# A decoder layer on one core: the queue model behind the emission order counts GpSimd's hold on VectorE and takes measured matmul times

## The chip, the cores and the metric

The kernel runs on one core of a Trainium2 chip. The metric is the device time of one execution in microseconds (us). The engines are named as the profile names them: PE (TensorE matmul) and PEld (its weight load), DVE (VectorE), ACT (ScalarE), POOL (GpSimd) and SP, which issues all the DMAs of this kernel. Each engine works through a queue of its own, in order; they meet only at semaphores.

## What is computed

One step of a decoder layer, for a prompt of 512 tokens and 8 samples that share the weights (520 columns). Cut to what matters:

```python
def mix_layer(x, ...):
    z = rms_norm(x, norm_g) @ w_in                  # 2048 x 7168, fp32
    u, gate_pool, qkv, gate_dil, q_mem, gate_mem = split(z)
    y_pool = pool_mix(u)                             # trailing means over 2/4/8/16, a 128x128 map per group
    for gi, (win, dil) in enumerate(((128, 1), (512, 4), (2048, 16))):
        q, k, v = rms_norm(q), rms_norm(k), v        # 4 heads in each of 3 groups
        o[gi], lse[gi] = dilated attention           # prompt: within 512 tokens; sample: over a cache
    y_dil = sum_g softmax_g(lse) * o                 # the groups of a head merged by their denominators
    y_mem = attention into 256 memory tokens         # its k and v come from mem @ w_mem_kv
    y = [silu(gate_pool)*y_pool | silu(gate_dil)*y_dil | silu(gate_mem)*y_mem]
    return x + y @ w_out                             # 1536 x 2048
```

The caches of the samples (88 MB) are copied to the outputs with one row added, from HBM to HBM.

## The kernel before

**Products in three parts.** Every fp32 product with a weight is made of three fp32r products, hi*hi, hi*lo and lo*hi. A column block of a weight (128 outputs) is a job; `run_jobs` (line 409) runs its 16 row blocks k (12 for w_out), each with three products over two halves of 260 columns, so six matmuls a step. The weights arrive in `wraw` tiles. `emit_split` (line 387) splits a quarter of a job (four row blocks): ACT rounds it to `whi` (line 154 of `act`) and DVE subtracts to get `wlo` (line 164 of `d_tt`). There are 304 such splits; they are counted here from 0. Five tiles of each kind exist (`SPB`, line 342), and a split is issued at the end of a quarter, three quarters ahead of its use, so that a `wlo` that DVE finishes late stops PE.

**Jobs.** In order: four of q_mem with the norm of x alongside; q and k of head 0 for two groups; eight of w_mem, with one half of 256 columns each (12 matmuls a quarter in place of 24); the gates; then for each head three v jobs and the q and k jobs of the next groups; the gate and the u of the pooled branch; and 16 of w_out, the first two of them together, k by k.

**Tasks.** All other work lies in generators: `norm_task` (line 501) of q and k, `mem_attn` (688), `dil_attn` (721), `sample_scores` (810), `sample_values` (833), `pool_task` (918). Each yields between steps. Sums and maxima over the 128 partitions are `partition_all_reduce` on POOL (`p_ar`, line 196): of squares `sq`, of a sample's scores `sk` (768 columns for a dilated unit, 512 for a memory one), of maxima and denominators `mx`.

**What sets the order.** The program is written out by a planner. `Clock` keeps a model of each engine's time: `use` (line 79) adds an instruction's estimated length to its engine, after what it reads and writes; the estimates stand in the helpers. After each row block `tick` (line 237) looks at the tasks in turn. A task's next step is emitted only when the model's PE has passed the time at which the step before is done, plus 1 us; nothing is emitted while the model has DVE or ACT more than 2.5 us ahead of PE in work (`busy`, line 234). So the estimates, not the chip, decide behind which split a step is put in the queue of its engine. For the first two w_out jobs `need_split` (line 1184) drives the tasks until the part of y that block k reads is split.

Names in the rows below: `sk`, `sv` are a sample unit's keys and values, `smx` its maximum, `sz` its denominator, `ss` and `sy` small tiles of the same unit, `qk` a q or k tile, `S` the prompt's scores of a head, `y4` to `y7` the gated outputs of the four dilated heads, `y0` to `y3` the gates of the pooled branch, `xl` and `xh` the two parts of x and later of y, `vn` a tile of v or of the residual x.

Of the kernel before, what the change touches and what calls it, by code (L numbers as in the profile page):

```python
# [10 lines left out]
F32 = mybir.dt.float32  # L11
# [37 lines left out]
class Clock:  # L49


    LAT = 0.12

    def __init__(self):
        self.pe = 0.0
        self.free = {"act": 0.0, "dve": 0.0, "pool": 0.0, "sp": 0.0, "hbm": 0.0}
        self.last = 0.0
        self.written = {}
        self.used = {}

    def after(self, ins, outs):
        t = 0.0
        for a in ins:
            t = max(t, self.written.get(a.tensor.name, 0.0))
        for a in outs:
            t = max(t, self.used.get(a.tensor.name, 0.0))
        return t
# [8 lines left out]
            self.written[n] = t  # L76
        self.last = max(self.last, t)

    def use(self, eng, dur, ins, outs):
        if eng == "pe":  # L80
            dep = max([self.written.get(a.tensor.name, 0.0) for a in ins])
            self.pe = max(self.pe, dep) + dur
            end = self.pe
            for a in ins:
                n = a.tensor.name
                self.used[n] = max(self.used.get(n, 0.0), end)
            for a in outs:
                n = a.tensor.name
                self.written[n] = max(self.written.get(n, 0.0), end + self.LAT)
                self.used[n] = max(self.used.get(n, 0.0), end)  # L90
            self.last = max(self.last, end + self.LAT)
            return
        end = max(self.free[eng], self.after(ins, outs)) + dur
        self.free[eng] = end
        self.done(end + self.LAT, ins, outs)

    def dma(self, nbytes, ins, outs):
        s = max(self.free["sp"], self.after(ins, outs)) + 0.57
        self.free["sp"] = s
        end = max(self.free["hbm"], s + 0.8) + nbytes / 345e3  # L100
        self.free["hbm"] = end
        self.done(end + 3.0, ins, outs)
# [5 lines left out]
def nfree(ap):  # L108
    n = 1
    for s in ap.shape[1:]:  # L110
        n *= s
    return n


def trunk(ctx, tc, nc, I, O):
    ck = Clock()
# [64 lines left out]

    def d_red(out, in_, op, axis):
        nc.vector.tensor_reduce(out=out, in_=in_, op=op, axis=axis)  # L183
        ck.use("dve", nfree(in_) * 0.00104 + 0.08, [in_], [out])

    def d_ttr(out, in0, in1, op0, op1, init, accum):
        nc.vector.tensor_tensor_reduce(out=out, in0=in0, in1=in1, scale=1.0, scalar=init, op0=op0, op1=op1,  # L187
# [3 lines left out]

    def d_recip(out, in_):
        nc.vector.reciprocal(out=out, in_=in_)
        ck.use("dve", nfree(out) * 0.0083 + 0.08, [in_], [out])

    def p_ar(t, op=RADD):
        nc.gpsimd.partition_all_reduce(t, t, P, op)  # L197
        ck.use("pool", nfree(t) * 0.00625 + 0.35, [t], [t])

    def p_tt(out, in0, in1, op):  # L200
        nc.gpsimd.tensor_tensor(out=out, in0=in0, in1=in1, op=op)
# [2 lines left out]
    def mm(out, lhsT, rhs, start, stop):  # L204
        nc.tensor.matmul(out, lhsT=lhsT, rhs=rhs, start=start, stop=stop)  # L205
        n = nfree(rhs)
        d = 2 * max(0.107, n / 1200.0) if lhsT.dtype == F32 else max(0.107, (n + 6) / 2400.0)
        ck.use("pe", d, [lhsT, rhs], [out])

    def tr(out, in_):  # L210
# [198 lines left out]
    def run_jobs(group, each=None, before=None):  # L409
# [13 lines left out]
        for k in range(nkb):  # L423
            if before:
                before(k)
            for j in group:
                _, _, lhs, sections, _, _ = jobs[j]
                if k % 4 == 0:
                    cur[j] = split_t.pop((j, k))
                whi, wlo = cur[j]  # L430
                mh, ml = lhs(k)
                for a, b, w, m in ((0, 0, whi, mh), (0, 1, whi, ml), (1, 0, wlo, mh)):
                    for s, (c0, c1) in enumerate(sections):
                        mm(accs[j][s], w[:, k % 4, :], m[:, c0:c1],
                           start=(k == 0 and a == 0 and b == 0), stop=(k == nkb - 1 and a == 1))
            if each:
                each(k)
            if k % 4 == 3:
                for _ in group:
                    emit_split()  # L440
            if flags.get("x"):
                while pend and (flags.get("mem") or pend[0][0]):
                    pend.pop(0)[1]()
            tick()
# [24 lines left out]
    def run_last(j):  # L469

        t = psum_m()
        xr = xres.pop(j - first_o)
        o = row("tmp", 3)
        for s, (c0, c1) in enumerate(SEC):
            acc = t[:, s, 0:c1 - c0]
            for k in range(KO):
                whi, wlo = split_t[j, k - k % 4]
                mh, ml = xs(k)
                for n, (w, m) in enumerate(((whi, mh), (whi, ml), (wlo, mh))):
                    mm(acc, w[:, k % 4, :], m[:, c0:c1], k == 0 and n == 0, k == KO - 1 and n == 2)  # L480
                if k == 0:
                    flush_pend()
            d_tt(o[:, c0:c1], acc, xr[:, c0:c1], ALU.add)
            store(O["o_y"][j - first_o][:, c0:c1], o[:, c0:c1])
# [16 lines left out]
    def norm_task(z, w, gcol, after):  # L501

        yield from take("sq")
        sq = row("sq", 2)[:, 0:w]
        act(sq, z, AF.Square)
        yield
        p_ar(sq)
        yield
        yield from rsqrt_steps(sq, P)
        d_stt(z, z, gains_r[:, gcol - GC_DQ:gcol - GC_DQ + 1], sq, ALU.mult, ALU.mult)  # L510
        give("sq")
        yield
        after()
# [174 lines left out]
    def mem_attn(h):  # L688
# [10 lines left out]
        d_tt(m, a[1], s[:, 0, :], ALU.max)  # L699
        yield  # L700
        p_ar(m, RMAX)
        yield
        d_tt(s[:, 0, :], s[:, 0, :], m, ALU.subtract)
# [9 lines left out]
        for kk in range(2):  # L713
            mm(o, vmem[h][:, kk * P:(kk + 1) * P], s[:, kk, :], kk == 0, kk == 1)
        yield
        p_ar(u)
        yield
        yield from finish_y(Y[8 + h][:, 0:SEQ], o, u)
# [131 lines left out]
    def sample_mem(h, bq, kx, vx):  # L850
        bs = slice(2 * bq, 2 * bq + 2)
        kv = kx.rearrange("p (b j) -> p b j", b=2)
        vv = vx.rearrange("p (b j) -> p b j", b=2)
        mx = st([P, 2], "smx", 2)
        z = st([P, 2], "sz", 2)
        y = st([P, 2], "sy", 2)
        d_red(mx, kv, ALU.max, AX.X)
        d_ts(mx, mx, -SCALE, ALU.mult)
        yield
        for b in range(2):  # L860
            act(kv[:, b, :], kv[:, b, :], AF.Exp, scale=SCALE, bias=mx[:, b:b + 1], accum=z[:, b:b + 1])
        yield
        d_recip(z, z)
        for b in range(2):
            d_ttr(vv[:, b, :], vv[:, b, :], kv[:, b, :], ALU.mult, ALU.add, 0.0, y[:, b:b + 1])
        d_tt(ysm[:, h, bs], y, z, ALU.mult)
# [3 lines left out]
    def sample_self(h):  # L870
        ss = st([P, NG, NS], "ss", 2)
        nself = st([P, NS], "nself", 2)
        d_tt(ss, qs[:, h], cs[:, :, :, 0, h], ALU.mult)
        yield
        p_ar(ss.rearrange("p g b -> p (g b)"))
        yield
        d_red(nself, ss.rearrange("p g b -> p b g"), ALU.max, AX.X)
        d_ts(nself, nself, -SCALE, ALU.mult)
        yield
        selfs[h] = (ss, nself)  # L880

    def sample_dil(h, bq, kx, vx):
        ss, nself = selfs[h]
        bs = slice(2 * bq, 2 * bq + 2)
        kv = kx.rearrange("p (g b j) -> p g b j", g=NG, b=2)
        vv = vx.rearrange("p (g b j) -> p g b j", g=NG, b=2)
        mx = st([P, 2], "smx", 2)
        z = st([P, 2], "sz", 2)
        zs = st([P, 2], "szs", 2)
        y = st([P, 2], "sy", 2)  # L890
        y2 = st([P, 2], "sy2", 2)
        d_red(mx, kv.rearrange("p g b j -> p b g j"), ALU.max, AX.XY)
        d_stt(mx, mx, -SCALE, nself[:, bs], ALU.mult, ALU.min)
        yield
        for b in range(2):
            act(kv[:, :, b, :], kv[:, :, b, :], AF.Exp, scale=SCALE, bias=mx[:, b:b + 1], accum=z[:, b:b + 1])
            c = 2 * bq + b
            act(ss[:, :, c], ss[:, :, c], AF.Exp, scale=SCALE, bias=mx[:, b:b + 1], accum=zs[:, b:b + 1])
        yield
        d_tt(z, z, zs, ALU.add)  # L900
        d_recip(z, z)
        d_tt(ss[:, :, bs], ss[:, :, bs], cs[:, :, bs, 1, h], ALU.mult)
        d_red(y2, ss[:, :, bs].rearrange("p g b -> p b g"), ALU.add, AX.X)
        for b in range(2):
            d_ttr(vv[:, :, b, :], vv[:, :, b, :], kv[:, :, b, :], ALU.mult, ALU.add, y2[:, b:b + 1], y[:, b:b + 1])
        d_tt(y, y, z, ALU.mult)
        ys = Y[4 + h][:, SEQ + 2 * bq:SEQ + 2 * bq + 2]
        d_tt(ys, ys, y, ALU.mult)
# [124 lines left out]
    for g, (w, d) in enumerate(WINS):  # L1033
        a, n, e = D2D[g]
# [292 lines left out]
```

## Time and profile before

| | |
|---|---|
| median of 3 runs | 927.62 us (927.02 to 927.92) |
| profiled execution, device time | 927.79 us |
| its span, first to last instruction | 926.0 us |
| mean granted clock | 0.992 |
| PE busy | 894.7 us (97%) |
| DVE busy | 672.9 us (73%) |
| ACT busy | 388.2 us (42%) |
| POOL busy | 285.0 us (31%) |

The profiled execution lies 0.2 us above the median of the runs, and its span 1.8 us below its device time. The table's shares are means over stages with different limits. What counts is where PE, the engine with hardly a gap, does stop, and on which engine's queue the thing stands that it waits for.

### The profile page before, as it was taken

To read this page: it belongs to the slowest core of one execution; us is meant where nothing else is said; L and a number is where in the kernel's file an instruction comes from. 1 tells how busy PE (TensorE), PEld (TensorE's weight loads), DVE (VectorE), ACT (ScalarE), POOL (GpSimd) and SP (SyncE) were. 2 spreads that over 40 slices of the span, in tenths; PEclk is the share of its full clock that TensorE was granted. 3 is DMA by queue.
4 is the path that set the end of the run, shared out by engine and by line. 5 is a ranking of instruction groups with operands and counts; after the bars stand their busy time and mean duration, and the time that the engine had idled before them with its cause. 6 is when DMAs were issued, how large, how long until landed. Compare 5 with 4: busy or idle time off the path is not lost.

```text
span 926.0 us, 17968 instructions
## 1 busy us (share of the span) xinstructions
PE 894.7 (97%) x7208; PEld 879.2 (95%) x7208; DVE 672.9 (73%) x1225; ACT 388.2 (42%) x795; POOL 285.0 (31%) x96
## 2 busy tenths in 40 slices
PE   7999898999999999999999999989999999999998
PEld 7999888999999999999998999989999899999998
DVE  7678999757888769977698866997659698333231
ACT  7547655443364434444343353245432624222220
POOL 1032544325444424622255322552215220000000
PEclk9999999999999999999999999999999999999999
DMA  9435346897877866578866788668975545899531
GB/s 347 157 114 196 115 154 224 270 341 233 275 222 258 289 223 212 195 260 311 289 233 217 271 300 311 218 221 285 332 253 195 211 137 197 329 389 352 196 104 47
DMA packets 64211, 219.52 MB, mean 237 GB/s; under 512 B 8440, under 2 KB 22648, under 8 KB 61944
## 3 DMA queue, kind: packets, MB, share of 16 engines
q1 hardware_dynamic: 64128, 218.39, 68.4%
q8 instruction: 56, 0.92, 0.4%
q14 instruction: 27, 0.22, 0.1%
HBM read 200.32 MB, written 106.25 MB: 331 GB/s over the span
## 4 chain that ended last, share of the span: by engine, by line
PE 70%; DVE 22%; ACT 3%; issue 3%; DMA 2%; POOL 0%; SPq 0%; DVEq 0%; ACTq 0%
PE psm L205 62%; PE psb L205 8%; DVE wlo L164 7%; DVE sv L187 3%; DVE mx L164 2%; DVE S L164 2%; DVE smx L183 1%; DVE sk L164 1%; ACT whi L154 1%; ACT sk L154 1%; DVE tmp L168 1%; DMA o_kv<-vt 1%; DVE vt L164 1%; DVE qk L164 1%; DVE smx L168 1%
## 5 line engine op out<-in xcount | busy, mean ns | idle before, releaser
L205 PE MATMUL psm<-xh,whi 128*128 128x260 f32 x2088 | 434.0, 288 | 9.2 <-ACT whi L154 8.4
L205 PE MATMUL psm<-xh,wlo 128*128 128x260 f32 x2088 | 426.2, 285 | 9.7 <-DVE wlo L164 9.7
L205 PE MATMUL psm<-xl,whi 128*128 128x260 f32 x2088 | 423.9, 284 | 0.0
L205 PEld LDWEIGHTS psm<-xh,whi 128*128 128x128 f32 x2088 | 326.2, 190 | 16.1 <-ACT whi L154 8.6
L164 DVE TENSOR_TENSOR wlo<-wraw,whi 128x512 fp32r<-128x512 f32 x304 | 270.4, 906 | 96.5 <-ACT whi L154 96.1
L205 PEld LDWEIGHTS psm<-xh,wlo 128*128 128x128 f32 x2088 | 324.8, 190 | 12.1 <-DVE wlo L164 12.0
L205 PEld LDWEIGHTS psm<-xl,whi 128*128 128x128 f32 x2088 | 324.4, 190 | 0.0
L154 ACT ACTIVATE whi<-wraw 128x512 fp32r<-128x512 f32 x304 | 181.0, 621 | 169.0 <-PE psm L205 149.3
L197 POOL PARTITION_ALL_REDUCE sk<-sk x32 | 130.3, 4071 | 130.3 <-DVE sk L164 56.1
L197 POOL PARTITION_ALL_REDUCE sq<-sq x32 | 101.0, 3164 | 186.2 <-ACT sq L154 186.2
L154 ACT ACTIVATE sk<-sk,smx 128x256 f32<-128x256 f32 (+1 forms) x64 | 35.5, 555 | 115.3 <-DVE smx L168 64.8
L197 POOL PARTITION_ALL_REDUCE mx<-mx x17 | 46.4, 2729 | 69.7 <-DVE mx L164 69.3
L164 DVE TENSOR_TENSOR tmp<-psm,vn 128x260 f32<-128x260 f32 x30 | 11.5, 424 | 76.8 <-PE psm L205 58.5
L154 ACT ACTIVATE tmp<-tmp 128x520 f32<-128x520 f32 (+2 forms) x76 | 46.3, 610 | 23.8 <-DVE sq L168 16.5
L154 ACT ACTIVATE sq<-qk 128x520 f32<-128x520 f32 x28 | 17.7, 636 | 85.9 <-DVE qk L164 77.9
L205 PE MATMUL psb<-y,wlo 128*128 128x256 f32 x128 | 37.7, 295 | 6.9 <-DVE wlo L164 6.9
L205 PE MATMUL psb<-y,whi 128*128 128x256 f32 x192 | 42.6, 290 | 0.8 <-ACT whi L154 0.8
L154 ACT ACTIVATE tmp<-sq,eps 128x520 f32<-128x520 f32 (+1 forms) x32 | 22.3, 696 | 33.2 <-POOL sq L197 33.2
L205 PEld LDWEIGHTS psb<-y,whi 128*128 128x128 f32 x192 | 32.9, 196 | 1.0 <-ACT whi L154 1.0
L187 DVE CUSTOM_DVE_ANT_1 sv<-sv,sk,sy 128x384 f32<-128x384 f32 x32 | 33.1, 1071 | 0.6
L205 PEld LDWEIGHTS psb<-y,wlo 128*128 128x128 f32 x128 | 24.9, 194 | 8.9 <-DVE wlo L164 8.8
L168 DVE SCALAR_TENSOR_TENSOR tmp<-sq,tmp 128x520 f32<-128x520 f32 (+1 forms) x32 | 21.6, 675 | 11.6 <-ACT tmp L154 11.6
(129 smaller groups left out, 740.8 us busy)
## 6 DMA issues: line engine op xcount, KB each, us to landing
o_cache<-cache SPq DMA_DIRECT2D x88, 712.0 KB, 7.9
wraw<-w_in SPq DMA_DIRECT2D x104, 512.0 KB, 5.3
o_cache<-cache SPq DMA_DIRECT2D x24, 584.0 KB, 6.6
vn<-xT SPq DMA_DIRECT2D x32, 260.0 KB, 5.7
wraw<-w_mem SPq DMA_DIRECT2D x16, 512.0 KB, 4.0
wraw<-w_out SPq DMA_DIRECT2D x14, 512.0 KB, 6.5
o_zero<-zero SPq DMA_DIRECT2D x6, 1024.0 KB, 8.8
sk<-dks SPq DMA_DIRECT2D x16, 384.0 KB, 3.0
```

Of the source, the lines that this page charges most:

```text
L154: nc.scalar.activation(out=out, in_=in_, func=func, scale=scale, bias=bias, **kw)
L164: nc.vector.tensor_tensor(out=out, in0=in0, in1=in1, op=op)
L168: nc.vector.scalar_tensor_tensor(out=out, in0=in0, scalar=scalar, in1=in1, op0=op0, op1=op1)
L183: nc.vector.tensor_reduce(out=out, in_=in_, op=op, axis=axis)
L187: nc.vector.tensor_tensor_reduce(out=out, in0=in0, in1=in1, scale=1.0, scalar=init, op0=op0, op1=op1, accum_out=accum)
L197: nc.gpsimd.partition_all_reduce(t, t, P, op)
L205: nc.tensor.matmul(out, lhsT=lhsT, rhs=rhs, start=start, stop=stop)
```

## The change

Three things in the planner's model; no instruction is added or taken away, and no tile changes its size.

1. `hold` is new. Each `p_ar` tells the model a stretch in which POOL's sum holds DVE: from 0.00563 us a column plus 0.1 us ahead of the sum's end, to 1.15 us ahead of it. If the model's DVE still has work queued at the stretch's start, the stretch's length is added to its time; an instruction that would start inside the stretch starts at its end. Reductions, reciprocals and instructions that read PSUM (tiles named `ps...`) are let through.
2. The length of a sum is 0.00563 us a column plus 0.35 us, before 0.00625 us.
3. A matmul of n columns takes n * 0.000456 + 0.0015 us in the model, before (n + 6) / 2400. For 260 columns that is 0.1201 us, before 0.1108 us.

```diff
     def use(self, eng, dur, ins, outs, shared=True):
...
-        end = max(self.free[eng], self.after(ins, outs)) + dur
+        start = max(self.free[eng], self.after(ins, outs))
+        if eng == "dve" and shared and not any(a.tensor.name.startswith("ps") for a in ins):
+            for s, e in self.held:
+                if s <= start < e:
+                    start = e
+        end = start + dur
         self.free[eng] = end
         self.done(end + self.LAT, ins, outs)
+
+    def hold(self, s, e):
+
+        if s < self.free["dve"]:
+            self.free["dve"] += e - s
+        self.held = [h for h in self.held if h[1] > self.pe] + [(s, e)]
...
     def p_ar(t, op=RADD):
         nc.gpsimd.partition_all_reduce(t, t, P, op)
-        ck.use("pool", nfree(t) * 0.00625 + 0.35, [t], [t])
+        ck.use("pool", nfree(t) * 0.00563 + 0.35, [t], [t])
+        e = ck.free["pool"]
+        ck.hold(e - nfree(t) * 0.00563 - 0.1, e - 1.15)
...
-        d = 2 * max(0.107, n / 1200.0) if lhsT.dtype == F32 else max(0.107, (n + 6) / 2400.0)
+        d = 2 * max(0.107, n / 1200.0) if lhsT.dtype == F32 else max(0.107, n * 0.000456 + 0.0015)
```

Of the 305 stretches of DVE's queue between two splits, 200 hold other instructions than before or hold them in another order; on ACT it is 147. Three places show how. Lines 164, 168, 179 and 183 of before are lines 177, 181, 192 and 196 of after.

DVE in the first dilated head, before, from split 137 (`wlo_751`) to split 139 (`wlo_764`):

```order
L164 TENSOR_TENSOR wlo_751_4897<-wraw_682_4381,whi_750_4896 128x512
L168 SCALAR_TENSOR_TENSOR tmp_749_4880<-sq_735_4786,tmp_749_4880 128x520
L168 SCALAR_TENSOR_TENSOR sq_735_4786<-tmp_749_4880,tmp_748_4879 128x520
L168 SCALAR_TENSOR_TENSOR qk_734_4783<-qk_734_4783,gains_r_3_66,sq_735_4786 128x520
L164 TENSOR_TENSOR wlo_754_4931<-wraw_697_4469,whi_753_4930 128x512
L164 TENSOR_TENSOR qk_756_4941<-psm_733_4776,rsx_9_72 128x260 x2
L183 TENSOR_REDUCE smx_758_4952<-sk_722_4681 128x2
L168 SCALAR_TENSOR_TENSOR smx_758_4952<-smx_758_4952,nself_674_4310 128x2
L179 COPY qs_19_82<-qk_734_4783 128x8
L164 TENSOR_TENSOR wlo_764_4973<-wraw_697_4469,whi_763_4972 128x512
```

After, from split 137 (`wlo_746`) to split 139 (`wlo_754`), and the first instruction behind it:

```order
L177 TENSOR_TENSOR wlo_746_4869<-wraw_682_4382,whi_745_4868 128x512
L177 TENSOR_TENSOR wlo_750_4908<-wraw_695_4461,whi_749_4907 128x512
L177 TENSOR_TENSOR qk_752_4918<-psm_730_4760,rsx_9_72 128x260 x2
L177 TENSOR_TENSOR wlo_754_4940<-wraw_695_4461,whi_753_4939 128x512
L177 TENSOR_TENSOR sz_736_4819<-sz_736_4819,szs_737_4820 128x2
```

The three steps of a norm (`tmp`, `sq`, `qk`) and the maximum of a sample unit (`smx`) no longer stand between these splits; both come behind split 141. The unit's values (`sz`, `sv`, `sy`), which stood ahead of split 137, now begin behind 139.

ACT at the gates of the pooled branch, before, from split 242 (`whi_1248`) to split 243 (`whi_1252`):

```order
L154 ACTIVATE whi_1248_8901<-wraw_1187_8436 128x512
L154 ACTIVATE sk_1216_8659,sz_1244_8883<-sk_1216_8659,smx_1243_8882 128x3x128
L154 ACTIVATE ss_1188_8439,szs_1245_8884<-ss_1188_8439,smx_1243_8882 128x3
L154 ACTIVATE sk_1216_8659,sz_1244_8883<-sk_1216_8659,smx_1243_8882 128x3x128
L154 ACTIVATE ss_1188_8439,szs_1245_8884<-ss_1188_8439,smx_1243_8882 128x3
L154 ACT_TABLE_LOAD
L154 ACTIVATE y0_1184_8409<-y0_1184_8409 128x520
L154 ACTIVATE y1_1205_8576<-y1_1205_8576 128x520
L154 ACTIVATE y2_1231_8752<-y2_1231_8752 128x520
L154 ACTIVATE y3_1251_8912<-y3_1251_8912 128x520
L160 ACT_TABLE_LOAD
L154 ACTIVATE whi_1252_8942<-wraw_1187_8436 128x512
```

After, from split 242 (`whi_1243`) on, with split 243 (`whi_1247`) in the second row:

```order
L167 ACTIVATE whi_1243_8890<-wraw_1192_8451 128x512
L167 ACTIVATE whi_1247_8923<-wraw_1192_8451 128x512
L167 ACTIVATE whi_1255_8961<-wraw_1201_8537 128x512
L167 ACTIVATE whi_1257_8992<-wraw_1201_8537 128x512
L167 ACTIVATE sk_1221_8718,sz_1251_8949<-sk_1221_8718,smx_1250_8948 128x3x128
L167 ACTIVATE ss_1185_8420,szs_1252_8950<-ss_1185_8420,smx_1250_8948 128x3
L167 ACTIVATE sk_1221_8718,sz_1251_8949<-sk_1221_8718,smx_1250_8948 128x3x128
L167 ACTIVATE ss_1185_8420,szs_1252_8950<-ss_1185_8420,smx_1250_8948 128x3
L167 ACTIVATE whi_1260_9028<-wraw_1213_8610 128x512
L167 ACTIVATE whi_1264_9069<-wraw_1213_8610 128x512
L167 ACTIVATE whi_1267_9100<-wraw_1218_8679 128x512
L167 ACT_TABLE_LOAD
```

Four exponentials of a sample unit and the two table loads with the four gates between them stood ahead of split 243. Now splits 243 to 245 come ahead of the exponentials, and 246 to 248 ahead of the table load.

DVE near the end of the w_mem jobs, before, from split 62 (`wlo_354`) to split 63 (`wlo_360`):

```order
L164 TENSOR_TENSOR wlo_354_1988<-wraw_306_1732,whi_353_1987 128x512
L168 SCALAR_TENSOR_TENSOR tmp_351_1969<-sq_325_1838,tmp_351_1969 128x256
L168 SCALAR_TENSOR_TENSOR sq_325_1838<-tmp_351_1969,tmp_350_1968 128x256
L168 SCALAR_TENSOR_TENSOR kmem0_11_74<-kmem0_11_74,gains_r_3_66,sq_325_1838 128x256
L164 TENSOR_TENSOR vt_356_1998<-psb_336_1890,mx_10_73 128x256
L164 TENSOR_TENSOR wlo_360_2017<-wraw_306_1732,whi_359_2016 128x512
```

After, around split 63 (`wlo_357`):

```order
L196 TENSOR_REDUCE smx_348_1968<-sk_297_1676 128x2
L187 TENSOR_SCALAR smx_348_1968<-smx_348_1968 128x2
L177 TENSOR_TENSOR vt_355_1983<-psb_333_1879,mx_10_73 128x256
L177 TENSOR_TENSOR wlo_357_1996<-wraw_307_1735,whi_356_1995 128x512
L177 TENSOR_TENSOR wlo_360_2014<-wraw_312_1773,whi_359_2013 128x512
L181 SCALAR_TENSOR_TENSOR tmp_352_1974<-sq_325_1830,tmp_352_1974 128x520
L181 SCALAR_TENSOR_TENSOR sq_325_1830<-tmp_352_1974,tmp_351_1973 128x520
L181 SCALAR_TENSOR_TENSOR qk_246_1387<-qk_246_1387,gains_r_3_66,sq_325_1830 128x520
```

The norm of a memory key (`tmp`, `sq`, `kmem0`), which stood ahead of split 63, comes behind split 67; the norm of a `qk` that had been done by split 58 now stands behind split 64.

## Rows read from the trace of the kernel before

**Rows 1.** Page: busy us (share), instructions; granted clock by slice, in tenths.

```profile
PE 894.7 (97%) x7208; PEld 879.2 (95%) x7208; DVE 672.9 (73%) x1225; ACT 388.2 (42%) x795; POOL 285.0 (31%) x96
...
PEclk9999999999999999999999999999999999999999
```

**Rows 2.** What PE waited for: total us, times, longest.

```profile
PE psm L205 <- DVE wlo L164: 9.7, 9, 2.6
PE psm L205 <- ACT whi L154: 8.4, 2, 6.2
PE psb L205 <- DVE wlo L164: 6.9, 8, 1.8
PE psb L205 <- ACT S L154: 1.6, 3, 0.9
```

**Rows 3.** Windows: us, busy PE, PEld, DVE, ACT, POOL; clock, DMA, GB/s.

```profile
104.00:158.00 54.00, 46.23 (x357) 44.10 (x356) 51.25 (x79) 30.80 (x65) 28.30 (x10) 0.97 0.53 174
158.00:362.00 204.00, 204.00 (x1619) 196.18 (x1618) 157.27 (x307) 86.05 (x190) 87.26 (x29) 1.00 0.78 257
362.00:416.00 54.00, 50.77 (x413) 49.76 (x412) 48.13 (x86) 24.67 (x56) 22.97 (x6) 1.00 0.69 234
416.00:478.00 62.00, 62.00 (x515) 61.74 (x514) 44.20 (x76) 24.51 (x52) 22.13 (x7) 1.00 0.78 271
478.00:534.00 56.00, 52.41 (x413) 51.35 (x413) 48.65 (x86) 24.10 (x55) 23.12 (x6) 0.97 0.74 254
594.00:626.00 32.00, 28.54 (x227) 27.96 (x226) 30.53 (x57) 12.82 (x32) 15.84 (x4) 0.98 0.64 229
705.00:757.00 52.00, 49.31 (x385) 48.20 (x384) 43.19 (x90) 22.17 (x52) 17.28 (x4) 0.97 0.58 198
```

**Rows 4.** Chain that ended last, in order of time: start, us, what.

```profile
163.21 46.13 PE psm L205 x384
```

**Rows 5.** Timeline, POOL, 380:402: start, us, instruction [idle before <-releaser].

```profile
387.86 4.67 POOL L197 PARTITION_ALL_REDUCE sk<-sk  x1 [0.64 <-POOL sq L197]
```

**Rows 6.** Timeline, DVE, same stretch.

```profile
381.20 0.69 DVE L168 SCALAR_TENSOR_TENSOR y<-y,mx 128x512 f32<-128x512 f32 x1
...
384.07 2.16 DVE L168 SCALAR_TENSOR_TENSOR smx<-smx,nself 128x2 f32<-128x2 f32 x1
386.15 0.68 DVE L164 TENSOR_TENSOR wlo<-wraw,whi 128x512 fp32r<-128x512 f32 x1
386.75 0.94 DVE L164 TENSOR_TENSOR sk<-sk,qs 128x768 f32<-128x768 f32 x1
388.75 3.04 DVE L164 TENSOR_TENSOR wlo<-wraw,whi 128x512 fp32r<-128x512 f32 x1 [1.05 <-ACT whi L154]
...
392.36 0.62 DVE L187 CUSTOM_DVE_ANT_1 sv<-sv,sk,sy 128x384 f32<-128x384 f32 x1
...
394.44 0.69 DVE L168 SCALAR_TENSOR_TENSOR tmp<-sq,tmp 128x520 f32<-128x520 f32 x1
...
395.90 0.76 DVE L168 SCALAR_TENSOR_TENSOR qk<-qk,gains_r,sq 128x520 f32<-128x520 f32 x1
...
397.85 0.94 DVE L183 TENSOR_REDUCE smx<-sk 128x2 f32<-128x768 f32 x1
```

**Rows 7.** Timeline, PE, same stretch.

```profile
391.85 0.51 PE L205 MATMUL psm<-xh,wlo 128*128 128x260 f32 x2 [1.34 <-DVE wlo L164]
```

**Rows 8.** Timeline, ACT, 715 to 757.

```profile
731.54 0.62 ACT L154 ACTIVATE sk<-sk,smx 128x384 f32<-128x384 f32 x1 [7.52 <-DVE smx L168]
...
733.42 1.28 ACT L154 ACT_TABLE_LOAD   x1
...
738.25 2.72 ACT L154 ACTIVATE whi<-wraw 128x512 fp32r<-128x512 f32 x5
```

**Rows 9.** Timeline, DVE, 120 to 160.

```profile
154.81 0.48 DVE L168 SCALAR_TENSOR_TENSOR kmem<-kmem,gains_r,sq 128x256 f32<-128x256 f32 x1
```

**Rows 10.** Timeline, PE, 786 to 792.

```profile
788.67 1.04 PE L205 MATMUL psb<-vt,kmem 128*128 128x260 f32 x4
```

**Rows 11.** Timeline, DVE, 786 to 812.

```profile
790.94 0.70 DVE L164 TENSOR_TENSOR xl<-y,xh 128x520 fp32r<-128x520 f32 x1 [0.70 <-ACT xh L154]
...
807.78 0.76 DVE L164 TENSOR_TENSOR tmp<-psm,vn 128x260 f32<-128x260 f32 x2 [12.57 <-DMA vn<-xT]
```

More of the change, by code (lines that the diff above doesn't have):

```diff
@@ L59, in __init__ @@
         self.used = {}
+        self.held = []
     def after(self, ins, outs):
@@ L77, in done, with use @@
         self.last = max(self.last, t)
-    def use(self, eng, dur, ins, outs):
+    def use(self, eng, dur, ins, outs, shared=True):
         if eng == "pe":
@@ L183, in d_red @@
         nc.vector.tensor_reduce(out=out, in_=in_, op=op, axis=axis)
-        ck.use("dve", nfree(in_) * 0.00104 + 0.08, [in_], [out])
+        ck.use("dve", nfree(in_) * 0.00104 + 0.08, [in_], [out], False)
     def d_ttr(out, in0, in1, op0, op1, init, accum):
@@ L193, in d_recip @@
         nc.vector.reciprocal(out=out, in_=in_)
-        ck.use("dve", nfree(out) * 0.0083 + 0.08, [in_], [out])
+        ck.use("dve", nfree(out) * 0.0083 + 0.08, [in_], [out], False)
     def p_ar(t, op=RADD):
         nc.gpsimd.partition_all_reduce(t, t, P, op)
-        ck.use("pool", nfree(t) * 0.00625 + 0.35, [t], [t])
+        ck.use("pool", nfree(t) * 0.00563 + 0.35, [t], [t])
+        e = ck.free["pool"]
+        ck.hold(e - nfree(t) * 0.00563 - 0.1, e - 1.15)
     def p_tt(out, in0, in1, op):
```

## The prediction

> **What bounds the kernel now.** I read the busy shares first: PE is busy 894.7 of 926.0 us at the full granted clock in every slice [rows 1], so 31.3 us of its idle time is all that any change of order can win. PE's own waits come next [rows 2]: DVE's `wlo` 9.7 and 6.9 us, ACT's `whi` 8.4 us (6.2 of it the start, which the change does not touch), the exponentials `S` 1.6 us. Then I looked for the stretches in which they lie. The windows [rows 3], width less PE busy, give A (104 to 158, the w_mem jobs) 7.8 us, B (362 to 416, dilated head 0) 3.2, C (478 to 534, head 1) 3.6, D (594 to 626, head 2) 3.5, E (705 to 757, head 3 and the gates) 2.7; together 20.7 us. Between them PE has no gap at all, and there DVE is busy 157.3 of 204 us and 44.2 of 62, while it is busy 51.3 of 54, 48.1 of 54, 48.7 of 56, 30.5 of 32 and 43.2 of 52 in A to E. So the kernel is bound by PE, except in five stretches where DVE's queue is full and has room in the next one.
>
> Why the queue is full shows in one spot of B. A `wlo` takes 0.68 us; the one at 388.75, with a sum of 4.67 us on POOL under way since 387.86 [rows 5], takes 3.04, and PE stands 1.34 us for it [rows 6, 7]. A step of two columns, `smx`, takes 2.16 us in the same way. The planner before counts nothing for that: it thinks the queue shorter than it is and puts more into it. It also has PE at 0.1108 us a product, where 384 products took 46.13 us, 0.1201 each [rows 4].
>
> **The change part by part.** No instruction is added or removed, so each engine's work is the same; only its place moves. *The matmul time* alone lets fewer products pass in a given model time, so it alone would put tasks earlier. *The hold* does the opposite. It gives a sum of 768 columns 0.00563 x 768 + 0.35 = 4.67 us, which is the row [rows 5], and a held stretch from 0.25 us after its start to 1.15 us before its end, 3.3 us. In the row the held `wlo` ends at 391.79, so its own 0.68 us began at 391.1, 1.4 us before the sum's end at 392.53: the hold is about 3.2 us. What wins can be read from the order alone: I count, ahead of each split that PE waited for, which DVE instructions no longer stand there.
>
> *B, C, D, E.* In B, behind split 139 now come, and before it no more: a norm (0.69 + 0.70 + 0.76), a maximum (0.94), three steps on `mx` and `y` (0.69 each), and a unit's values (two of 0.62 and eight short ones of 0.1 to 0.2) [rows 6]; that is 2.15 + 0.94 + 2.07 + 2.4 = 7.5 us, against 2.8 us that PE had lost by then. At the last split of B that PE waits for, 143, it is a norm and a unit's values, 4.7 us against 3.2 lost. The same count gives, in C, 3.1 us ahead of split 171 (2.0 lost by then) and 4.7 at 179 (3.6 lost); in D, 6.8 at 207 (3.5 lost), three `mx` and `y` steps, a `y` product, a maximum, a product `sk` (0.94) and a unit's values; in E, 2.9 at 243 (2.4 lost) and 4.9 at 247 (2.7 lost). In each the work taken out exceeds the loss, so the queue reaches the split before PE does. E has a second cause, on ACT: it waits 7.52 us for a `smx`, then loads tables, and its five `whi` start only at 738.25 [rows 8]; after, three splits pass ahead of that wait and three more ahead of the tables, so `whi` no longer queues there. The exponential of a sample unit now stands 5.1 us of products behind its maximum on average, before 2.5 (64 instructions; products between them times 0.12 us). I take all 13.0 us of B to E as gone. What is late next is the far product of a dilated head, which stands 1.4 us of products behind the exponential `S` in all four heads, before 1.4 to 2.2; but `S` has its maximum 15 to 17 us ahead, before 9 to 14, so it should be done early. I set 1.0 us for such new waits, between 0 and 3.6, four times the 0.9 us that the largest wait for `S` cost.
>
> The work lands where DVE has room: after B the window 416 to 478 has 17.8 us free for 4.7. If that cover were gone, the 4.7 us would stop PE one for one.
>
> *A.* Here a quarter is 12 products, 1.4 us, of which one `wlo` takes half. Ahead of split 63, the last that PE waits for, stand a norm of a `qk` (2.15 us) and the norm of a memory key (3 x 0.42 to 0.48 [rows 9]) and a copy less, a maximum of a memory unit (0.8) more: 2.8 us. DVE is behind through all of A, so PE's loss falls by that: 7.8 to 5.0. Bounds: nothing, because further up the change goes the wrong way (ahead of split 49 stand 1.9 us more, a unit's product and values), and 4.1, if two key sums of 256 columns that also leave A no longer hold DVE, some 0.65 us each by the excess of such a `wlo` over its 0.68 us. I take 2.8, the count.
>
> *The end.* Behind E only w_out follows. There DVE waits 12.57 us for a residual tile that comes by DMA [rows 11], PE 0.8 us after it; the DMAs keep their order, so I take nothing, between a loss of 2 us and a gain of 0.8.
>
> *Sum.* 927.8 (the profiled execution) - 2.8 - 13.0 + 1.0 = 913.0 us; on the median of the runs, 0.2 us lower, the same within rounding.
>
> *A rule against it.* The held `wlo` ran on 1.4 us before the sum ended [rows 5, 6]. The Trainium skill, page "SBUF — State Buffer", section "SBUF: two separate sides", says that the port pair shared by VectorE and GpSimd is locked, and whichever instruction started first keeps it to its end. By that rule the model still undercounts each sum by 1.15 us; by the row it does not. What the time would be by the rule is the second rival.
>
> **The rivals.**
>
> *1. Half stays (about 920).* The stalls of B to E may come less from the length of DVE's queue than from chains through POOL and ACT: ACT stands still for 7.52 us behind one `smx` [rows 8], and every such wait delays the `whi` behind it. For it: such waits exist in each head. Against: the distances have doubled. It gives half of B to E, 6.5, and half of A: 927.8 - 6.5 - 1.4 = 919.9.
>
> *2. The hold is still undercounted (about 917).* If sums held DVE to their end, five sums in a head's stretch would hide 5 x 1.15 = 5.8 us from the planner, and the 4.7 us taken out would leave 1.1 us in each of the four: 913.0 + 4.3 = 917.3. Against: the row.
>
> *3. It does nothing (926 to 929.6).* The two corrections oppose each other, and A, where both meet, shows it: 1.9 us more ahead of one split, 2.8 less ahead of another. If the same held in B to E, the stalls would only move. Against: the counts there all have one sign.
>
> *4. Slower: the pooled branch arrives late at w_out (over 930).* The last part of y is split for block 11 of the first two w_out jobs. Its product stood before at block 5 and stands now at block 8. From the product's start at 788.67 [rows 10] to the end of the last `xl` at 791.64 [rows 11] it takes 3.0 us. Between the product and its use now lie 36 products, 36 x 0.12 = 4.3 us, before 72. With the product's own 1.0 us not counted, 1.9 us of chain stand against 4.3: it is 2.4 us early. Each us that DVE is later than that stops PE for one; from 17.2 us late (2.4 + 14.8, the gain) the kernel is slower than before. For it: the pooled branch's steps now crowd splits 252 to 261. Against: no sum runs on POOL there, so nothing holds DVE. With the whole 20 us that six such late tasks could take, it gives 913.0 + 17.6 = 930.6.
>
> **How the numbers follow.** The forecast (910 to 916.5) has 0.57, rival 1 0.14, rival 2 0.13, rival 3 0.09, rival 4 0.07. About 0.2%, 1.9 us, is what a measurement of this kernel can tell from no change. Faster is the forecast with rivals 1 and 2, 0.84; same 0.09; slower 0.07. The lower end is all of A's 4.1 us, no new waits, and the end's 0.8 us: 927.8 - 4.1 - 13.0 - 0.8 = 909.9, and I go to 909. Upwards the range takes in rivals 1 and 2 with 1 us to spare: 921. What it leaves out are rivals 3 and 4, 0.16.
>
> **What would show each step.** PE's busy time should stay at 894 to 896 us, and its idle time fall from 31 to about 16.5. PE's waits for `wlo` should fall from 16.6 us to 5 or 6, nearly all in A; the wait for `whi` to the 6.2 us of the start. In B to E the windows should show PE busy all through, and DVE less busy there, busier in the stretches behind. Held `wlo` of 2 to 3 us should still be there, since the sums still run: only PE no longer waits for them. ACT's wait of 7.52 us for a `smx` ahead of the five `whi` should no longer stand ahead of a `whi` that PE needs. The prediction is wrong if PE stops in B to E for more than 4 us in all, if A loses as much as before, or if PE stops at block 10 or 11 of the first w_out jobs.

## The result, and the profile after

The changed kernel takes 905.49 us (median of four executions, 903.43 to 907.41), before it was 927.70 us: a ratio of 0.9761, with a 95% interval of 0.9739 to 0.9784. That is 22.2 us faster, where 14.8 us were forecast, and below the low end of the range, 909. The profiled execution took 905.43 us, its span is 903.7 us, its mean granted clock 0.996 (before 0.992).

The page of after, busy time and granted clock by slice, answers to [rows 1]:

```profile
PE 885.6 (98%) x7208; PEld 874.5 (97%) x7208; DVE 660.9 (73%) x1225; ACT 392.0 (43%) x795; POOL 287.4 (32%) x96
...
PEclk9999989999999999999999999999999999999999
```

Two terms can be read from it. PE's idle time, span less busy, fell from 31.3 to 903.7 - 885.6 = 18.1 us, by 13.2. And PE's **busy** time fell from 894.7 to 885.6 us, by 9.1, with the same 7208 instructions. The prediction had said that it stays.

What PE waited for, after (us in total, times, longest), answers to [rows 2]:

```profile
PE psb L220 <- DVE wlo L177: 7.8, 5, 4.2
PE psm L220 <- ACT whi L167: 6.4, 1, 6.4
PE psm L220 <- DVE tmp L177: 0.5, 1, 0.5
PE psm L220 <- DVE wlo L177: 0.3, 1, 0.3
```

Eight waits are left, where the whole view of before has 25. The waits of the wide jobs (`psm`) for `wlo` are gone but for 0.3 us, the 6.4 us of `whi` are the start, and the w_mem jobs (`psb`) keep all that they had. The windows A to E of after, with the columns of [rows 3]:

```profile
104.00:158.00 54.00, 46.20 (x362) 45.10 (x361) 50.38 (x78) 31.93 (x65) 25.47 (x8) 0.94 0.54 177
362.00:416.00 54.00, 54.00 (x449) 53.84 (x448) 48.56 (x90) 27.82 (x61) 25.80 (x7) 1.00 0.79 271
478.00:534.00 56.00, 56.00 (x465) 55.84 (x465) 43.33 (x79) 25.94 (x54) 26.42 (x7) 1.00 0.81 297
594.00:626.00 32.00, 32.00 (x266) 31.84 (x265) 31.44 (x49) 14.72 (x30) 19.42 (x5) 1.00 0.77 276
705.00:757.00 52.00, 52.00 (x425) 51.68 (x424) 45.25 (x107) 24.54 (x50) 8.93 (x2) 1.00 0.50 166
```

B to E have no idle time at all. (The work of after runs up to some 20 us ahead of before, so a window holds somewhat later work; but the waits above leave only 0.3 us of `wlo` outside the w_mem jobs, wherever the window lies.) In windows of the same width PE now runs 449, 465, 266 and 425 matmuls, before 413, 413, 227 and 385 [rows 3]: 167 more, and at 0.12 us each that is 20 us, not 13. A stands still for 7.8 us, as before.

The held steps are still there, and no longer in PE's way. In the timeline of DVE after, in the first dilated head, two `wlo` take 2.77 us under a sum (4.08 us on POOL, from 381.67), and PE waits for neither:

```profile
383.12 2.77 DVE L177 TENSOR_TENSOR wlo<-wraw,whi 128x512 fp32r<-128x512 f32 x2
```

**Where the 9.1 us of busy time come from.** The timeline of PE before, around the 1.97 us stall in C (the stretch of the kernel before that the prediction did not look at):

```profile
505.24 0.80 PE L205 MATMUL psm<-xh,wlo 128*128 128x260 f32 x2 [1.97 <-DVE wlo L164]
505.84 0.64 PE L205 MATMUL psm<-xh,whi 128*128 128x260 f32 x2
506.27 0.64 PE L205 MATMUL psm<-xl,whi 128*128 128x260 f32 x2
...
508.74 0.40 PE L205 MATMUL psm<-xl,whi 128*128 128x260 f32 x2
```

Behind the stall the pairs start 0.43 us apart instead of 0.24, until 508.7. The windows behind the four longest stalls of before (1.85, 1.97, 2.59 and 2.18 us) show the granted clock of it (last but two of the columns):

```profile
115.30:119.50 4.20, 4.19 (x22) 4.19 (x23) 4.13 (x7) 1.42 (x3) 0.00 (x0) 0.59 0.37 125
505.24:508.70 3.46, 3.46 (x16) 3.46 (x17) 3.46 (x3) 2.04 (x4) 2.49 (x1) 0.52 0.77 272
624.55:628.20 3.65, 3.62 (x17) 3.62 (x18) 2.85 (x5) 1.32 (x5) 0.43 (x1) 0.53 1.01 321
738.90:744.20 5.30, 5.27 (x29) 5.08 (x30) 5.19 (x8) 2.69 (x5) 2.88 (x1) 0.68 0.76 236
```

Near 0.5 is the lower of the two levels, 1.2 GHz. Each such stretch lost (1 - clock) x width, 1.7 us: 6.8 us in the four. After, one is left, behind the 4.17 us stall in A:

```profile
132.10:137.20 5.10, 5.10 (x25) 5.10 (x26) 3.43 (x7) 0.87 (x2) 0.00 (x0) 0.52 0.70 212
```

It lost 0.48 x 5.1 = 2.4 us, so the clock gave back 6.8 - 2.4 = 4.4. The rest is the restart. The rows of before around the stall of [rows 7]:

```profile
390.11 0.40 PE L205 MATMUL psm<-xl,whi 128*128 128x260 f32 x2
391.85 0.51 PE L205 MATMUL psm<-xh,wlo 128*128 128x260 f32 x2 [1.34 <-DVE wlo L164]
392.19 0.40 PE L205 MATMUL psm<-xh,whi 128*128 128x260 f32 x2
```

Running, a pair starts 0.24 us after the one ahead of it. The pair behind the gap takes 0.51 us in place of 0.40, and the gap counts only from the end of the matmul ahead, which lasts 0.28 us by its record while the next would have started 0.12 after it. So 0.11 + 0.16 = 0.27 us of each stall count as busy. Seventeen stalls fewer give 4.6 us. 4.4 + 4.6 = 9.0 of the 9.1 us. The 0.27 is read from one stall here; the end of the section on stalls of a chosen length puts it to all profiles.

### The profile page after: what moved, and what is told of

Its sections match the earlier page's. It is cut to its first block, busy times and chain, and to the rows that moved or that the text cites. A ratio compares the mean times of both kernels' runs of the same rounds, so it can differ in the third digit from the quotient of the medians.

```text
span 903.7 us, 17969 instructions
## 1 busy us (share of the span) xinstructions
PE 885.6 (98%) x7208; PEld 874.5 (97%) x7208; DVE 660.9 (73%) x1225; ACT 392.0 (43%) x795; POOL 287.4 (32%) x96
## 4 chain that ended last, share of the span: by engine, by line
PE 94%; DVE 3%; DMA 1%; issue 1%; ACT 0%; SPq 0%; DVEq 0%; ACTq 0%
PE psm L220 82%; PE psb L220 11%; DVE wlo L177 1%; DMA vn<-xT 1%; PE psb L226 1%; DVE sq L181 0%; DMA gains<-gains 0%; DVE sv L200 0%; DVE tmp L181 0%; DVE qs L192 0%; DVE tmp L177 0%; DVE sk L177 0%; DVE smx L196 0%; SPq L230 0%; DVE kmem L177 0%
## 5 line engine op out<-in xcount | busy, mean ns | idle before, releaser
L177 DVE TENSOR_TENSOR wlo<-wraw,whi 128x512 fp32r<-128x512 f32 x304 | 257.4, 862 | 72.0 <-ACT whi L167 70.6
L167 ACT ACTIVATE whi<-wraw 128x512 fp32r<-128x512 f32 x304 | 184.6, 624 | 255.4 <-PE psm L220 200.5
L210 POOL PARTITION_ALL_REDUCE sq<-sq x32 | 103.8, 3254 | 129.7 <-ACT sq L167 124.4
L177 DVE TENSOR_TENSOR qk<-psm,rsx 128x260 f32<-128x260 f32 x56 | 21.3, 421 | 21.4 <-PE psm L220 21.4
L167 ACT ACTIVATE tmp<-sq,eps 128x520 f32<-128x520 f32 (+1 forms) x32 | 22.2, 695 | 25.0 <-POOL sq L210 25.0
L196 DVE TENSOR_REDUCE smx<-sk 128x2 f32<-128x512 f32 (+1 forms) x32 | 26.0, 812 | 6.6 <-POOL sk L210 6.6
```

What stands on the lines that cost most here:

```text
L167: nc.scalar.activation(out=out, in_=in_, func=func, scale=scale, bias=bias, **kw)
L177: nc.vector.tensor_tensor(out=out, in0=in0, in1=in1, op=op)
```

## The experiments

The theory on the change (theory 1) is that the hold freed B to E. The theory on the size (theory 2) is that a stall costs its gap, 0.27 us of restart, and behind some of the longer ones a slow stretch. Ratios are against the kernel before on the same chip; of the first four runs it took 927.05 us, of the three stalls 927.68, of the last two 926.90.

### The matmul time alone

```diff
# in the kernel before
-        d = ... max(0.107, (n + 6) / 2400.0)
+        d = ... max(0.107, n * 0.000456 + 0.0015)
```

> The kernel before with the third part of the change alone: a matmul of 260 columns is 0.1201 us in the model, and sums hold nothing. Theory 1 (the hold is what freed the splits in B to E; the matmul time alone lets fewer products pass per model time, so steps come earlier into DVE's queue): slower than before, 930 to 945 us, PE idle in B to E well over the 13.0 us of before, waits for wlo up from 16.6 us. Rival (the measured matmul time is what put the model right): faster than before, 905 to 918 us. Under 0.2% of difference would say that it does nothing alone.

938.46 us, ratio 1.0121 (1.0106 to 1.0136): slower, as theory 1 has it. PE waits in more places than before, and the steps that come earlier block other things too (`vt`, a v tile that DVE takes out of PSUM only behind a unit's values):

```profile
PE psm L205 <- ACT whi L154: 11.3, 4, 6.6
PE psb L205 <- DVE wlo L164: 7.6, 7, 2.2
PE psm L205 <- DVE wlo L164: 5.3, 5, 2.3
PE psb L211 <- DVE vt L164: 5.0, 4, 4.0
```

The expected sign of `wlo` was wrong in one point: these waits fell from 16.6 to 12.9 us, while those for `whi`, `vt` and `S` rose. PE's idle time in B to E is 15.7 us (windows 362:416, 478:534, 594:640, 705:760), 2.7 more than before and not well over it; A, with what now runs over its end (104 to 170), loses 11.1 us, before 7.8. The truer matmul time, put in by itself, costs 11 us.

### The hold alone

```diff
# in the changed kernel
-        d = ... max(0.107, n * 0.000456 + 0.0015)
+        d = ... max(0.107, (n + 6) / 2400.0)
```

> The changed kernel with the old matmul time, 0.1108 us for 260 columns; hold and the length of the sums as changed. Theory 1 (the hold does it): B to E stay free of waits (under 1 us of PE idle, before 13.0), 900 to 910 us; steps come later still than in the changed kernel, so PE's idle time in the w_mem jobs (7.8 us) may fall by some us, and something may be late at the first w_out jobs. Rival (both parts are needed; alone the hold leaves half of the waits, or puts off so much that w_out waits for it): over 915 us.

907.20 us, ratio 0.9778 (0.9762 to 0.9795), nearly all of the gain. The new length of the sums, the second part of the change, is in this run too; no run has it apart. PE is busy in B to E all through. Its waits, without the start and two of 0.5 us:

```profile
PE psb L220 <- DVE wlo L177: 4.4, 5, 1.6
PE psb L220 <- DVE y L181: 2.4, 1, 2.4
PE psm L220 <- DVE tmp L177: 2.1, 2, 1.6
```

A loses less (4.4 us of `wlo`, no slow stretch), but a pooled product now waits 2.4 us for `y`, and w_out stops 1.6 us for a `tmp`: the steps are later, as expected. In the changed kernel, where the measured matmul time lets them come sooner, both waits are absent. Between the two kernels lie 1.7 us, and the intervals overlap. What no run shows is whether a plain delay of all steps, blind to where the sums stand, would have freed B to E as well.

### The hold up to the sum's end

```diff
# in the changed kernel
-        ck.hold(e - nfree(t) * 0.00563 - 0.1, e - 1.15)
+        ck.hold(e - nfree(t) * 0.00563 - 0.1, e)
```

> The changed kernel, with the held stretch reaching to the sum's end instead of 1.15 us before it. Theory 1 (on the chip DVE goes on some 1.2 to 1.4 us before the sum's end, so 1.15 us for each of some 87 sums, 100 us of model time, would be counted that never pass; the model then thinks DVE late all the time and puts steps off until w_out waits for them): slower than the changed kernel, 910 to 940 us, with PE's waits in the first w_out jobs. Rival (the port pair is held to the sum's end, so this is the truer model): the same as the changed kernel or faster, 895 to 905 us. The Trainium skill, page 'SBUF — State Buffer', section 'SBUF: two separate sides', states the rival's rule.

948.35 us, ratio 1.0229 (1.0213 to 1.0244): 43 us slower than the changed kernel and beyond the 910 to 940 us that theory 1 gave. PE's idle time is 52.9 us, 34.8 more than in the changed kernel, and its busy time 893.5, 7.9 more. The two longest of its waits stand at the first two w_out jobs (a third, 6.3 us for a `whi`, stands in the w_mem jobs):

```profile
780.84 2.10 PE L220 MATMUL psb<-vt,kmem 128*128 128x260 f32 x4 [9.51 <-DVE y L181]
...
811.38 0.80 PE L220 MATMUL psm<-xh,whi 128*128 128x260 f32 x2 [21.30 <-ACT xh L167]
```

The first wait is for the step that writes a gated output of the pooled branch. What the second waited for stands in ACT's timeline:

```profile
810.70 2.75 ACT L167 ACTIVATE xh<-y 128x520 fp32r<-128x520 f32 x5 [2.28 <-DVE y L177]
```

That `y` (128x2, done at 810.66) is the last step of a dilated sample unit, and the units of the last head still have sums on POOL until 805.3. A model that thinks DVE later than it is puts steps off, and the last ones stand in front of w_out, which needs y split (`xh`). This is like rival 4 of the prediction, work that comes late at w_out, but the larger part is not the pooled branch that rival 4 names: it is the samples of the last dilated head.

The rule of the Trainium skill (page "SBUF — State Buffer", section "SBUF: two separate sides"), that the port pair is kept to the end of the instruction, is by the record not what this kernel's sums do. In the changed kernel's timeline of POOL two sums follow each other:

```profile
122.90 3.64 POOL L210 PARTITION_ALL_REDUCE sk<-sk  x1 [9.04 <-DVE sk L177]
126.44 3.36 POOL L210 PARTITION_ALL_REDUCE sq<-sq  x1
```

And DVE under them, with the `wlo` of split 49 as the first of the two in the last row (a norm of 2.2 us, from 129.20, stands ahead of it):

```profile
123.33 2.25 DVE L192 COPY qs<-qk 128x8 f32<-128x8 f32 x1
...
126.16 0.40 DVE L200 CUSTOM_DVE_ANT_0 sv<-sv,sk 128x256 f32<-128x256 f32 x1
...
126.49 2.58 DVE L200 CUSTOM_DVE_ANT_0 sv<-sv,sk 128x256 f32<-128x256 f32 x1
...
131.34 1.29 DVE L177 TENSOR_TENSOR wlo<-wraw,whi 128x512 fp32r<-128x512 f32 x2
```

The copy, 0.16 us by itself, ends at 125.58, so it began 1.1 us before its sum's end at 126.54; the second `sv`, 0.40 by itself, began at 128.67, 1.1 us before 129.80. Whether a sum gives the port pair back early, or its record runs on past its last access, no run shows; for the planner it is the same.

### Nothing but the memory keys in the w_mem jobs

```diff
# in the changed kernel; "hot" is set at the first w_mem job and cleared behind the last
+        while flags.get("hot") and w == NT:        # norm_task
+            yield
-            while i not in s_k:                    # sample_scores
+            while i not in s_k or flags.get("hot"):
```

> The changed kernel; while the eight w_mem jobs run, no sample unit's scores and no norm of a q or k tile are started, so that DVE has the splits and the memory keys alone. Theory 2 (a stall of PE costs more than its gap: the gap, some 0.27 us because the first two matmuls behind it take 0.51 us instead of 0.24, and behind the longest ones a stretch at 1.2 GHz worth some 2 to 2.7 us): A gives back 7.8 + 5 x 0.27 + 2.4, about 11 us: 893 to 897 us, PE busy 882 to 884 us, and the runs agree within 1 us since no stall is left that may or may not lower the clock. Rival (the gap is all that a stall costs): 897 to 899 us with PE busy 885 to 886 us. Other rival (the work put off stops PE in the next stretches or at w_out): 902 us or more.

894.98 us (894.38 to 895.52), ratio 0.9651 (0.9637 to 0.9666): the fastest version of this study, 10.5 us below the changed kernel. Its page:

```profile
PE 881.7 (99%) x7208; PEld 871.4 (98%) x7208; DVE 662.0 (74%) x1225; ACT 392.9 (44%) x795; POOL 286.1 (32%) x96
```

And its window A:

```profile
104.00:158.00 54.00, 53.85 (x454) 53.65 (x453) 36.10 (x60) 30.86 (x63) 16.95 (x7) 1.00 0.58 190
```

Idle time fell by 18.1 - (892.6 - 881.7) = 7.2 us and busy time by 3.9, to a granted clock of 1.000. So the gap is not all that a stall costs: that rival had 897 to 899 and PE busy at 885. Theory 2's own figures (11 us, PE busy 882 to 884) were close (10.5 and 881.7 came); the term of 0.27 us was put there as two matmuls of 0.51 instead of 0.24, which is right in its sum alone, as shown above.

### Only the sample scores paused

The same edit without that of `norm_task`.

> The changed kernel with only the sample scores paused during the w_mem jobs; the norms of q and k run there as in the changed kernel. Theory 2 (a sum on POOL and the values of a unit are what stood ahead of split 49, where PE lost 4.17 us): A keeps under 2 us of idle time and no slow stretch: 896 to 899 us. Rival (the norms are the load): 901 us or more.

898.67 us, ratio 0.9694 (0.9679 to 0.9708). A keeps 3.0 us of idle time and no slow stretch:

```profile
104.00:158.00 54.00, 51.01 (x423) 49.96 (x422) 48.12 (x68) 32.04 (x63) 23.55 (x9) 1.00 0.59 189
```

The sample units are most of A's loss (905.49 to 898.67), the norms the rest (to 894.98). The idle time left was put too low by 1 us. The norms were not paused apart, so the shares are those of this order.

### The pause in the kernel before

The pause of both, in the kernel before, whose model has no hold.

> The kernel before, with its old model, and only the pause of sample scores and q/k norms during the eight w_mem jobs (as in the run e4_quiet_w_mem). Theory 2 with independent stages: A gives back its gaps, restarts and its slow stretch, 7.8 + 9 x 0.27 + 1.7, less a short rest, 9 to 11 us: 916 to 919 us; B to E keep their 13 us of idle time and their three slow stretches. Rival (what is put off from A comes back in B to E, which have no hold in their model): 921 us or more, PE's idle time in B to E above 15 us.

921.39 us, ratio 0.9935 (0.9918 to 0.9951): neither text is right. The time is the rival's, if only just (the interval, 919.3 to 922.4 us, reaches below its 921), the place is not. A gains 5.2 us of busy time, but PE now stops behind it, where before it had no gap [rows 3]:

```profile
104.00:158.00 54.00, 51.42 (x424) 50.31 (x423) 43.08 (x72) 31.48 (x66) 23.54 (x9) 1.00 0.62 200
300.00:362.00 62.00, 58.44 (x471) 56.69 (x470) 57.10 (x109) 24.71 (x55) 29.83 (x10) 1.00 0.66 229
```

Of the 62 - 58.4 = 3.6 us in 300 to 362, 1.7 are two stalls that were not there before (0.53 at 308.4 and 1.17 at 327.1), and 1.9 are a wait for `S` at 357.4 that belongs to B (at 365.9 before, 0.5 us). B to E as a whole keep their loss, which the rival did not have: with the windows 6 us earlier, as the work now is, and the whole of that wait, 13.2 us, before 13.0; their three slow stretches stay too. A gave back less than theory 2 said, since 2.6 us of stalls remain in it, and what was put off cost 1.7 us ahead of B and some 0.8 more at the first w_out jobs, not in B to E. With the hold in the model the same pause gave 10.5 us, without it 5.5: the two changes do not simply add, and about half of the difference lies in A itself, where 0.15 us stay with the hold and 2.6 without it.

### One stall of a chosen length

```diff
# in the kernel before, ahead of split 290, in the middle of w_out (n = 16, 18, 21)
+        if i == 290:
+            for _ in range(n):
+                nc.vector.tensor_tensor(out=masks, in0=masks, in1=masks, op=ALU.max)
```

> The kernel before with 16 extra DVE steps of 128x512 ahead of split 290, in the middle of w_out, where DVE is idle two thirds of the time and the split is done some 9.9 us before PE needs it. It makes one stall of PE of about 0.5 to 1.5 us (16 steps of 0.66 to 0.72 us less 9.9). Theory 2 (a stall costs its gap, 0.27 us of slower first matmuls, and only behind long stalls a stretch at 1.2 GHz): the gap plus 0.3 us, no slow stretch behind it: 928.5 to 929.5 us. Rival (a stall costs its gap alone): the gap, PE busy unchanged at 894.7. Second rival (every stall brings a slow stretch): the gap plus 2 us.

> As the run with 16 steps, with 18: a stall of about 2 to 3 us. Theory 2: the gap plus 0.27 us plus a stretch at 1.2 GHz of some 16 matmuls, 0.21 us each instead of 0.12, about 1.5 to 2 us: 931 to 933 us, PE busy about 2 us over 894.7 and one more dip in the granted clock, at the place of the stall. Rival (the gap alone): 930 to 931 us, PE busy 894.7, no dip.

> As the run with 16 steps, with 21: a stall of about 4 to 5.2 us. Theory 2: the gap, 0.27 us and a slow stretch a little longer than behind the middle stall (the 4.17 us stall of the changed kernel's w_mem jobs was followed by 2.4 us of excess, those of 1.85 to 2.59 us in the kernel before by 1.7 to 2.1): 934 to 936 us. Rival (the gap alone): 932 to 933 us.

| steps | stall | time | more than before | ratio, 95% |
|---|---|---|---|---|
| 16 | 1.52 us | 929.92 us | 2.2 us | 1.0022 (1.0013 to 1.0032) |
| 18 | 2.98 us | 932.99 us | 5.3 us | 1.0057 (1.0041 to 1.0073) |
| 21 | 5.16 us | 934.81 us | 7.1 us | 1.0075 (1.0060 to 1.0091) |

With 16 steps, PE's timeline at the stall, and then the window behind it:

```profile
885.23 0.51 PE L205 MATMUL psm<-xh,wlo 128*128 128x260 f32 x2 [1.52 <-DVE wlo L164]
```

```profile
885.20:891.50 6.30, 6.27 (x52) 6.27 (x53) 3.74 (x9) 1.27 (x2) 0.00 (x0) 1.00 0.81 279
```

The same two views with 18 steps, the window of the stall itself ahead of the one behind it:

```profile
884.73 0.80 PE L205 MATMUL psm<-xh,wlo 128*128 128x260 f32 x2 [2.98 <-DVE wlo L164]
```

```profile
881.70:884.70 3.00, 0.05 (x1) 0.00 (x0) 2.90 (x6) 0.00 (x0) 0.00 (x0) 0.89 0.00 0
884.70:891.00 6.30, 6.27 (x29) 6.27 (x30) 3.06 (x6) 0.63 (x1) 0.00 (x0) 0.51 0.77 246
```

And with 21:

```profile
887.33 0.80 PE L205 MATMUL psm<-xh,wlo 128*128 128x260 f32 x2 [5.16 <-DVE wlo L164]
```

```profile
882.00:887.40 5.40, 0.24 (x3) 0.08 (x1) 5.20 (x9) 0.11 (x1) 0.00 (x0) 0.75 0.00 0
887.40:891.70 4.30, 4.30 (x20) 4.30 (x21) 2.95 (x6) 0.07 (x1) 0.00 (x0) 0.52 0.75 243
```

The short stall has no slow stretch behind it: 1.52 + 0.27 = 1.8 us, inside its interval (1.2 to 3.0 us), which doesn't tell it from the gap alone; the time lies 0.4 us above what was expected. Behind the middle one 0.49 x 6.3 = 3.1 us are lost, behind the long one 0.48 x 4.3 = 2.1 us: 2.98 + 0.27 + 3.1 = 6.3 (measured 3.8 to 6.8) and 5.16 + 0.27 + 2.1 = 7.5 (5.6 to 8.4). The gap alone lies below both of these intervals. The loss behind the middle stall, 3.1 us, is more than the 1.5 to 2 that were expected. And what theory 2 said of the longer stretch behind the longer stall did not come: it was the shorter one. The windows of the stalls show why. In both the clock fell while PE still stood, (1 - 0.89) x 3.0 = 0.3 us' worth in the middle stall and (1 - 0.75) x 5.4 = 1.35 in the long one; with 3.1 and 2.1 behind, it is 3.4 us in both. The longer stall has more of the same fall inside its gap, where it costs nothing. PE's busy time in single profiles (894.0, 895.9, 896.1) follows only roughly, since other stalls of these executions differ by a slow stretch or two.

All eleven profiles of this study test the 0.27 us better than the short stall does. Take from PE's busy time 0.27 us for each of its waits, and half of the time that it was busy at the lower clock: 894.7 - 25 x 0.27 - 6.8 = 881.2 us before, 885.6 - 8 x 0.27 - 2.4 = 881.0 after, 881.7 - 3 x 0.27 = 880.9 with the pause of both, 884.1 - 8 x 0.27 = 881.9 with that of the samples, 893.5 - 12 x 0.27 - 9.6 = 880.7 with the hold to the end. The eleven lie between 880.6 and 882.9 us, where the busy times as they stand spread over 17 us.

## Why the prediction was wrong, point by point

- **What bounds the kernel: right, with one misreading.** PE is the bound, stopped where DVE's queue is full; B to E were the right places. But "at the full granted clock in every slice" [rows 1] was wrong. A 9 means 90% or more of 23 us, and a stretch of 3.5 us at half clock hides in that. The signs stood in the rows quoted: clocks of 0.97, 0.97, 0.98 and 0.97 in A, C, D and E, against 1.00 between them [rows 3], and a first pair of 0.51 us [rows 7].
- **The hold against the matmul time: right.** The hold, with the new length of the sums, gives 907.2, the matmul time alone 938.5.
- **B to E, 13.0 us of idle time: right in place and size, wrong in price.** All of it is gone. This is the step that failed: the prediction priced a stall at its gap, "31.3 us of its idle time is all that any change of order can win", and had PE's busy time stay at 894 to 896 us. It fell to 885.6. With 12 stalls x 0.27 = 3.2 us and three slow stretches, 5.1 us, the same count gives 21.3 us for these four stages.
- **New waits, 1.0 us: none came.** PE waits for no `S` at all.
- **A, 2.8 us: wrong, no idle time was won.** "Nothing" was the prediction's own lower bound, and "if A loses as much as before" one of its signs of being wrong. I took the change of work ahead of split 63, the last that PE waited for before. The place that then mattered was split 49, where my own count had 1.9 us more: a held copy, a unit's values with 2.58 us of hold, and a norm stand ahead of its `wlo` at 131.34 (the DVE rows in the third experiment). PE lost 4.17 us there in one piece, and 1.81 at 147.7 for split 57; for none behind it did PE wait. In A the worst split decided, not the last one. The runs with the pause show that sample units and norms, not the splits themselves, are A's load.
- **The end: right within 0.5 us.** Its stalls fell from 1.3 to 0.8 us.
- **Rivals.** Half stays, and nothing: refuted by B to E. The hold undercounted by 1.15 us a sum: refuted by B to E too, where none of its 1.1 us a stage is left, and by the held steps, which start 1.1 to 1.4 us ahead of a sum's end; the run with the hold to the sum's end fits. The late pooled branch: it did not come with this change, but both neighbours of it show it, at 2.4 us (hold alone) and 9.5 us (hold too long, where 21.3 us more are the samples of the last dilated head).
- **The signs.** PE's waits for `wlo` fell to 8.1 us, nearly all in A, where 5 or 6 were said, and its idle time to 18.1, where 16.5 were said; A's 2.8 us, which were not won, account for it. That DVE would be less busy in B to E shows in C alone (43.3 us, before 48.7), in windows that hold later work than before.

The mended sum, made after the fact from the profiles of before and after: 927.8 - 13.0 - 3.2 - 5.1 (B to E) - 0.4 (A: four stalls fewer, 1.1, one slow stretch longer by 0.7) - 0.5 - 0.3 (the end) + 0.1 (the start) = 905.4 us; the profiled execution took 905.43. Against the forecast of 913.0, B to E gave 8.3 us more, the end 0.8 more and no new wait took the 1.0, while A gave 2.4 less: the errors partly cancel.

## What to carry to other kernels

Price a stall of PE by what follows it, too: read the granted clock of a window of a few us behind it, and compare the first pair of matmuls with the steady ones, before you add up gaps. A planner's estimates work together: correcting one of two that err in opposite directions cost 11 us here, and overstating the other by 1.15 us a sum cost 43. When work is moved, follow the worst split along the stage, not the last one. And put off work with care: what one stage is spared can stop PE elsewhere, as in front of w_out.

## What was not expected of the hardware

- Behind the same stall of 1.96 to 1.97 us in C, the clock fell in one execution and not in another. In the profile of before it fell (0.52). In the run with the middle stall, whose code is the same up to w_out, it did not, by the window behind the stall there:

```profile
505.50:509.00 3.50, 3.48 (x29) 3.48 (x30) 3.50 (x3) 2.07 (x4) 2.51 (x1) 1.00 1.00 321
```

and another stall, 1.28 us, follows there at 512.8. The other two runs of the group agree: in that with the short stall the clock stayed (1.00) and a stall of 1.30 us followed, in that with the long one it fell (0.57) and none did.

- This further stall is missing in the profile of before, too. The likely reason, not tested apart, is that slower matmuls give DVE time to catch up: where its queue is behind, a slow stretch is partly won back (1.7 us lost, 1.28 + 0.27 spared).
- The length of a stall alone does not tell whether the clock falls. In the run with the hold alone, a stall of 2.44 us ending at 768.3 has a clock of 1.00 behind it (768 to 772), and one of 1.62 us at 786.9, with 0.47 us more at 788.1, a clock of 0.50 (787.9 to 791.3). What does decide stays open here.
- The spread of the changed kernel goes with the clock: its four executions took 903.43, 905.43, 905.56 and 907.41 us at mean clocks of 0.998, 0.996, 0.996 and 0.994, 2 us for each 0.002. Without a stall that long (the run with the pause) four executions lie within 1.1 us.
- A sum over partitions lets DVE go 1.1 to 1.4 us before its end by the record: 1.1 twice in A, 1.4 in [rows 5, 6].
